# Dividing the attention outputs by their softmax sums after the products instead of before them

## Chip, cores and metric

One core of one Trainium2 chip runs the whole program. The metric is the device time of one execution in microseconds (us). The kernel before took 2548.91 us as the median of three runs (2546.77 to 2551.94).

## What is computed

A decoder trunk of two layers on 1024 positions and 1024 channels, in float32. Each layer projects the normalised input, runs 16 attention heads in three kinds (A: six heads with dilated windows, B: six heads with latent keys and values, C: four differential heads), projects the 1024 channels of all heads with `w_o`, adds the input, and ends with an up and a down projection. The part that matters here:

```python
for layer in range(DEPTH):
    ...
    out_a = mixer_dilated(qa, ka, va, cos64, sin64)
    out_b = mixer_mla(cq, ckv, kr, ...)
    out_c = mixer_diff(qc, kc, vc, ...)
    mixed = jnp.concatenate([out_a, out_b, out_c], axis=-1)
    x = x + mixed @ w_o[layer]
    u = rmsnorm(x, ln2_g[layer]) @ w_up[layer]
    x = x + jnp.square(jax.nn.relu(u)) @ w_down[layer]
```

For a head of kind A or B the output of query i is sum over j of exp(s_ij) v_j, divided by sum over j of exp(s_ij). The kernel computes A's mixture of three windows as one such softmax with a weighted mask.

## The kernel before

**Split products.** Every float32 matrix is split into a high and a low part of TensorE's float32 form (names with `h` and `l`: `mixh`, `mixl`, `ph`, `pl`, `h_wo`, `l_wo`), and a product is three matmuls: high x high, high x low, low x high. The splits keep ScalarE (ACT), GpSimd (POOL) and VectorE (DVE) busy beside TensorE (PE).

**Who sets the order.** The program is first recorded: every operation is noted with its tiles (L179). `order()` (L256) then schedules the noted operations with estimated costs (`cost`, L240); where an operation may run on more than one engine, `WAYS` (L50) lists them (s is ACT, g POOL, v DVE). `replay()` (L409) issues each engine's instructions in that order, so every instruction in the trace has the line L418. On one engine instructions run strictly in the issued order, and the queue of SyncE (SP), which issues all DMAs, is in order too. SBUF is divided into rings of slots per tag (`SLOTS`, L32): a tile takes the next slot of its tag and must wait until the tile that held it has been read. Tags spoken of here are `pp` (5 slots of 128x512), `ms`, `mx` and `oo` (2 slots each) and `pw` (5).

**The heads.** Heads run in the order A0, A1, C0 to C3, A2 to A5, B0 to B5 (`CHUNKS`, `units`), each in four groups of two 128-query blocks. `PLAN` places the other work of the layer beside them. For a query block, `scores` (L804) makes the scores on PE, a masked minimum on DVE (written to `p`, minimum in `w`), the exponential with its sum on ACT, a reciprocal of the sum on DVE (128x1), and the division of the whole row block `p` on POOL:

```python
nc.scalar.activation(p, p, AF.Exp, bias=w[:, z:z + 1], scale=-1.0, accum_out=tot)
if mi == 0:
    if coef is None:
        nc.vector.reciprocal(w[:, 3:4], tot)
        copy("norm", p, p, w[:, 3:4])
```

One group later `values` (L849) turns `p` on PE (`ptp`), splits it into `ph` (ACT) and `pl` (DVE), both in `pp`, and multiplies with the split values into a PSUM bank `o`, whose rows 0 to 63 and 64 to 127 hold two partial sums. `o_sum` (L892) copies both halves with ACT (64x512 each), adds them on POOL and stores the sum to `mix_dram`, twice per head.

While a pair of A heads runs, the keys and queries of the next pair are prepared: POOL multiplies and splits them (`tm_kA`, `tm_qA`), and PE turns them (`pt_kA`).

**The output projection.** Its input rows f = 0 to 7 (128 channels each, a pair of heads; 0 to 2 are A, 3 to 5 are B, 6 and 7 are C) are taken in the groups (6, 0), (7, 1), (2, 3, 4) and (5). `project_load` (L1195) loads the weights and, per f and half z, one 128x512 tile `mixr` from `mix_dram` into `pp`; POOL rounds it to `mixh`, DVE subtracts to `mixl`. The first two groups run beside the B heads. The last two follow the attention: for the first four row tiles t the sums `po_2` of all three f of group (2, 3, 4) are opened in eight PSUM banks, then f = 5 closes them; DVE adds them to `xr`.

```python
raw = tl("pp", [P, 512], f"mixr_{L}_{f}_{z}")
nc.sync.dma_start(raw, mix_dram[L * D + f * P:L * D + (f + 1) * P, cs])
hi_pool(mh[:, cs], raw)
lo_dve(ml[:, cs], raw, mh[:, cs])
```

Of the kernel before, what the change touches and what calls it, by code (L numbers as in the profile page):

```python
# [17 lines left out]
P = 128  # L18
S = 1024
# [27 lines left out]
LAG = 3  # L47
DEEP = 6000.0

WAYS = {'hi': 'g', 'hiact': 's', 'lo': 'vg', 'lop': 'g', 'evac': 'sv', 'norm': 'g', 'osum': 's', 'oadd': 'g', 'lsc': 'gs', 'rope': 'v', 'sq': 's', 'fadd': 'gv', 'fhi': 'sg', 'flo': 'vg', 'fnorm': 'sg', 'fevac': 'sv', 'fsnap': 's', 'fsq': 'sv'}  # L50
SHARED = 0.5

BLOCKS = (0, 4, 8, 12, 15)
# [368 lines left out]
def tile_trunk(  # L422
# [14 lines left out]
    def tl(tag, shape, name, dt=F32):  # L437
        assert 4 * math.prod(shape[1:]) <= SLOTS[tag][0]
        return nc.tile(pool, shape, dt, name, tag, SLOTS[tag][1])
# [25 lines left out]
    def copy(kind, o, i, scale=None):  # L465

        ways = []
        for z in WAYS[kind]:
            if z == "s":
                ways.append(("scalar", "activation", (o, i, AF.Copy), dict(scale=1.0 if scale is None else scale)))  # L470
            elif z == "v":
                ways.append(("vector", "tensor_copy", (o, i), {}) if scale is None else ("vector", "tensor_scalar", (o, i, scale, None, ALU.mult), {}))
            else:
                ways.append(("gpsimd", "tensor_scalar", (o, i, 1.0, 0.0, ALU.mult, ALU.add) if scale is None else (o, i, scale, 1.0, ALU.mult, ALU.mult), {}))
        nc.either(*ways)
# [46 lines left out]
    hl_dram = nc.tile(dram, [DEPTH * NT, P, D], F32, "hl_dram")  # L522
    cq_dram = nc.tile(dram, [DEPTH * S, 512], F32, "cq_dram")
    mix_dram = nc.tile(dram, [DEPTH * D, S], F32, "mix_dram")

    def rstd_of(y, ssq, n, eps, w, nm):

# [45 lines left out]
    for L in range(DEPTH):  # L573
# [153 lines left out]
        def mix_tile(f, g):  # L727
            if (f, g) not in mixf:
                mixf[f, g] = tl("mx", [P, 512], f"mix_{L}_{f}_{g}")
            return mixf[f, g]  # L730

        def mix_out(f, g, src, r0=0, n=P):

            nc.sync.dma_start(mix_dram[L * D + f * P + r0:L * D + f * P + r0 + n, g * 512:(g + 1) * 512], src)
# [69 lines left out]
        def scores(hd, g):  # L804

            maps, scale, nm = hd["maps"], hd["scale"], hd["nm"]
            hd["P"][g] = [None, None]
            cur = {}

            def piece(i, mi, z, c0, m):  # L810
                W = (i + 1) * P
                passes, coef = maps[mi]
                if c0 == 0:
                    cur["w"] = st(f"w_{nm}_{i}_{mi}")
                    cur["p"] = tl("pw", [P, W], f"p_{nm}_{i}_{mi}")
                w, p = cur["w"], cur["p"]
                s = bank("s", f"s_{nm}_{i}_{mi}_{c0}")
                n = max(256, m)
                for pi, (lq, rk) in enumerate(passes):
                    mm(s[:, 0:n], lq[:, i * P:(i + 1) * P], rk[:, c0:c0 + n], pi == 0, pi == len(passes) - 1)  # L820
                nc.vector.tensor_tensor_reduce(out=p[:, c0:c0 + m], in0=s[:, 0:m], in1=hd["mask"](W, c0, m), scale=-scale,
                                               scalar=w[:, 0:1] if z else BIG, op0=ALU.add, op1=ALU.min, accum_out=w[:, z:z + 1])
                if c0 + m < W:
                    return
                tot = hd["tot"][mi][:, i] if "tot" in hd else w[:, 2:3]
                nc.scalar.activation(p, p, AF.Exp, bias=w[:, z:z + 1], scale=-1.0, accum_out=tot)
                if mi == 0:
                    if coef is None:
                        nc.vector.reciprocal(w[:, 3:4], tot)
                        copy("norm", p, p, w[:, 3:4])  # L830
                    hd["P"][g][i % 2] = p
                else:

                    prev = hd["P"][g][i % 2]
                    nc.vector.reciprocal(w[:, 3:4], tot)
                    nc.vector.scalar_tensor_tensor(w[:, 4:5], w[:, 3:4], hd["tot"][0][:, i], coef, ALU.mult, ALU.mult)
                    nc.vector.scalar_tensor_tensor(prev, p, w[:, 4:5], prev, ALU.mult, ALU.add)

            bl = []
            for i in (2 * g, 2 * g + 1):  # L840
                for mi in range(len(maps)):
                    W = (i + 1) * P
                    cuts = [0, W] if W <= 512 else [0, hd.get("cut", 384), W] if W == 640 else [0, 512, W]
                    for z in range(len(cuts) - 1):
                        c0, m = cuts[z], cuts[z + 1] - cuts[z]
                        bl.append((len(maps[mi][0]) * max(256, m) * 0.42, lambda i=i, mi=mi, z=z, c0=c0, m=m: piece(i, mi, z, c0, m)))
            return bl
# [44 lines left out]
        def o_sum(g, o, f, par, nm):  # L892

            tmp = tl("oo", [P, 512], f"ot_{nm}_{g}")
            rows = slice(64 * par, 64 * par + 64)
            dst = tl("oo", [P, 512], f"od_{nm}_{g}")[rows, :] if f < 6 else mix_tile(f, g)[rows, :]
            copy("osum", tmp[rows, :], o[64:128, :])
            copy("osum", dst, o[0:64, :])
            pair("oadd", dst, dst, tmp[rows, :], ALU.add)
            if f < 6:  # L900
                mix_out(f, g, dst, 64 * par, 64)

        def fin_mix(f, par, nm):
            return lambda g, o: o_sum(g, o, f, par, nm)

        def mask_a(W, c0, m):
            return maska[:, S - W + c0:S - W + c0 + m]
# [7 lines left out]
        def prep_a(h):  # L915
            i, par = h // 2, h % 2
            qa, ka, va = heads[f"A{i}"]
            nm = f"A{L}{h}"
            c = slice(64 * par, 64 * par + 64)
            qs = tl("stk", [P, S], f"qs_{nm}", F32R)  # L920
            k1s = tl("stk", [P, S], f"k1s_{nm}", F32R)
            k2s = tl("stk", [P, S], f"k2s_{nm}", F32R)

            def two(src):
                def f(o, ts_):
                    hi_pool(o[:, :, 0:64], src[:, ts_, c])
                    lo_dve(o[:, :, 64:128], src[:, ts_, c], o[:, :, 0:64])
                return f

            def keys(cs, pt):  # L930
                hi_act(k1s[:, cs], pt)
                for z in range(2):
                    nc.sync.dma_start(k2s[64 * z:64 * z + 64, cs].bitcast(F32), k1s[64 - 64 * z:128 - 64 * z, cs].bitcast(F32))

            k = turned(f"k{nm}", two(ka), keys)
            q = turned(f"q{nm}", two(qa), lambda cs, pt: hi_act(qs[:, cs], pt))
            bl = zipped(k[0], k[1], q[0], q[1])
            return bl, dict(maps=[([(qs, k1s), (qs, k2s)], None)], mask=mask_a, scale=SC_A, nm=nm, P={},
                            v=make_v(va[:, :, c], par, nm), fin=fin_mix(i, par, nm))


        bx = {}
# [136 lines left out]
        def prep_b(h):  # L1079
            i, j = h // 2, h % 2  # L1080
            nm = f"B{L}{h}"
            qh, ql = [z[:96] for z in pairs[i][0][j]]
            kh, kl = [Halves(*z) for z in pairs[i][1][j]]
            return [], dict(maps=[([(qh, kh), (qh, kl), (ql, kh)], None)], mask=mask_c, scale=SC_B, nm=nm, P={}, cut=512,
                            v=make_v(bx["V"][:, :, 64 * h:64 * h + 64], j, nm), fin=fin_mix(3 + i, j, nm))

        cst = {}

# [106 lines left out]
        def project_load(gi):  # L1195

            ws, mx = [], []
            if gi == 0:
                for t in range(NT):
                    xs[t] = x_tile(t, f"xr_{L}_{t}")  # L1200
                    src = x[0] if L == 0 else xl_dram
                    nc.sync.dma_start(xs[t], src[t * P:(t + 1) * P, :])
            for f in groups[gi]:
                sc = cst["sg2"] if f >= 6 else None
                ws.append([split(w_o[L, f * P:(f + 1) * P, z * 512:(z + 1) * 512], f"wo_{L}_{f}_{z}", sc) for z in range(2)])
                tag = MIX[f]
                mh = tl(tag, [P, S], f"mixh_{L}_{f}", F32R)
                ml = tl(tag, [P, S], f"mixl_{L}_{f}", F32R)
                for z in range(2):
                    cs = slice(z * 512, (z + 1) * 512)  # L1210
                    raw = tl("pp", [P, 512], f"mixr_{L}_{f}_{z}")
                    nc.sync.dma_start(raw, mix_dram[L * D + f * P:L * D + (f + 1) * P, cs])
                    hi_pool(mh[:, cs], raw)
                    lo_dve(ml[:, cs], raw, mh[:, cs])
                mx.append((mh, ml))
            return ws, mx
# [503 lines left out]
```

## Time and profile before

| what | us |
|---|---|
| median of three runs | 2548.91 |
| the profiled execution | 2549.46 |
| its span in the trace | 2547.70 |
| PE busy | 2473.8 (97% of the span) |
| DVE busy | 2069.9 (81%) |
| ACT busy | 1238.3 (49%) |
| POOL busy | 920.2 (36%) |
| mean granted TensorE clock | 0.991 of full speed |

The span lies 1.76 us under the profiled execution's own time, and that execution 0.55 us over the median. Busy shares are averages over the whole program. A change in one stage is read from that stage's own window: how much of it PE was idle, what ended each idle stretch, and the granted clock there.

### The profile page before, as it was taken

The numbers are of one execution on the slowest core, as the hardware profiler recorded it, in microseconds if no ns is written. First come the engines' busy times: TensorE is split into PE (matmuls) and PEld (weight loads), VectorE is DVE, ScalarE is ACT, GpSimd is POOL, SyncE is SP. The second block draws the span as 40 slices with busy tenths as digits, with TensorE's granted clock in tenths as the row PEclk, the third lists the DMA queues.
The fourth block names the chain that finished last, engine by engine and source line by source line (L and its number), as shares of the span: only waits on it lengthen the run. The fifth ranks groups of instructions, "written<-read, shape, count | busy, mean of one in ns | idle before, by whom it ended". The sixth has DMA issues, their size and how long they took to land. (4 is left out here: it accounts for less than half of the span.)

```text
span 2547.7 us, 39227 instructions
## 1 busy us (share of the span) xinstructions
PE 2473.8 (97%) x12808; PEld 2077.0 (82%) x12808; DVE 2069.9 (81%) x4326; ACT 1238.3 (49%) x2548; POOL 920.2 (36%) x1078
## 2 busy tenths in 40 slices
PE   8999999999999999999999999999999999999996
PEld 7878889988788887888888778898887888788885
DVE  4679998887877777989856799988778777789989
ACT  3566667743544444323235666677345444333332
POOL 2344355653200114455323343556330001144543
PEclk9999999999999999999999999999999999999998
DMA  8354433433354457544453554344243444765332
GB/s 255 96 142 135 112 94 94 135 93 130 116 172 164 153 197 262 156 145 120 137 164 97 133 137 122 81 110 142 78 142 129 163 159 146 268 210 157 112 120 79
DMA packets 292636, 360.58 MB, mean 142 GB/s; under 512 B 48848, under 2 KB 172112, under 8 KB 292432
## 3 DMA queue, kind: packets, MB, share of 16 engines
q1 hardware_dynamic: 292432, 358.08, 45.6%
q8 instruction: 102, 1.67, 0.3%
q14 instruction: 102, 0.84, 0.1%
HBM read 231.63 MB, written 94.90 MB: 128 GB/s over the span
## 5 line engine op out<-in xcount | busy, mean ns | idle before, releaser
L418 PE MATMUL pd<-hb,ha 128*128 128x512 f32 x2520 | 577.2, 390 | 5.4 <-DVE hb L418 3.5
L418 PE MATMUL pu<-xc,uh 128*128 128x512 f32 x1792 | 552.7, 393 | 13.4 <-ACT ua L418 8.2
L418 PEld LDWEIGHTS pd<-hb,ha 128*128 128x128 f32 x2520 | 471.4, 188 | 109.6 <-DVE hb L418 8.3
L418 PEld LDWEIGHTS pu<-xc,uh 128*128 128x128 f32 x1792 | 336.9, 189 | 90.0 <-ACT ua L418 10.0
L418 PE MATMUL pu<-xc,ul 128*128 128x512 f32 x896 | 346.7, 393 | 0.0
L418 PEld LDWEIGHTS pu<-xc,ul 128*128 128x128 f32 x896 | 169.6, 189 | 36.8 <-DVE ul L418 0.8
L418 DVE TENSOR_TENSOR ha<-hr,ha 128x512 fp32r<-128x512 f32 x151 | 145.6, 967 | 24.8 <-POOL ha L418 23.0
L418 POOL TENSOR_SCALAR ha<-hr 128x512 fp32r<-128x512 f32 x90 | 74.1, 824 | 245.1 <-DVE xd L418 94.8
L418 ACT ACTIVATE hb<-wt 128x512 fp32r<-128x512 f32 x98 | 60.4, 627 | 184.4 <-PE pd L418 157.3
L418 ACT ACTIVATE uh<-su 128x512 fp32r<-128x512 f32 x124 | 77.5, 631 | 138.4 <-PE pu L418 121.6
L418 ACT ACTIVATE hb<-wd 128x512 fp32r<-128x512 f32 x82 | 50.4, 627 | 158.8 <-PE pd L418 157.3
L418 ACT ACTIVATE p_C<-p_C,w_C 128x256 f32<-128x256 f32 (+7 forms) x128 | 98.9, 773 | 55.3 <-DVE w_C L418 54.7
L418 POOL TENSOR_SCALAR p_A<-p_A,w_A 128x128 f32<-128x128 f32 (+3 forms) x96 | 77.2, 806 | 116.5 <-DVE w_A L418 83.6
L418 POOL TENSOR_SCALAR uh<-wu 128x512 fp32r<-128x512 f32 x16 | 13.3, 832 | 280.1 <-PE pu L418 168.5
L418 DVE TENSOR_TENSOR hb<-wt,hb 128x512 fp32r<-128x512 f32 x105 | 109.7, 1061 | 0.7 <-ACT hb L418 0.5
L418 DVE TENSOR_TENSOR xd<-pd,xd 128x512 f32<-128x512 f32 x128 | 86.8, 682 | 26.6 <-PE pd L418 26.5
L418 PE MATMUL pf_C<-wh_C,hh 128*128 128x512 f32 x256 | 104.7, 413 | 1.7 <-POOL wh_C L418 0.9
L418 PE MATMUL pf_C<-wl_C,hh 128*128 128x512 f32 x256 | 104.4, 408 | 0.4 <-DVE wl_C L418 0.3
L418 PE MATMUL po<-h_wo,mixh 128*128 128x512 f32 x256 | 103.3, 403 | 1.0 <-POOL h_wo L418 1.0
L418 POOL TENSOR_SCALAR p_B<-p_B,w_B 128x384 f32<-128x384 f32 (+4 forms) x96 | 74.4, 780 | 79.8 <-DVE w_B L418 62.3
L418 PE MATMUL pf_A<-wh_A,hh 128*128 128x512 f32 (+1 forms) x256 | 100.0, 395 | 3.0 <-DVE w_C L418 2.1
L418 PE MATMUL pf_C<-wh_C,hs_C 128*128 128x512 f32 x256 | 101.8, 401 | 0.7 <-DMA hs_C<-hl_dram 0.7
(343 smaller groups left out, 6775.8 us busy)
## 6 DMA issues: line engine op xcount, KB each, us to landing
hr<-hc_dram SPq DMA_DIRECT2D x210, 256.0 KB, 2.8
wu<-in_w_up_dram SPq DMA_DIRECT2D x148, 256.0 KB, 3.0
hc_dram<-hc SPq DMA_DIRECT2D x120, 256.0 KB, 2.3
wd<-in_w_down_dram SPq DMA_DIRECT2D x120, 256.0 KB, 3.7
hs_C<-hl_dram SPq DMA_DIRECT2D x32, 512.0 KB, 3.5
hs_A<-hl_dram SPq DMA_DIRECT2D x32, 512.0 KB, 3.5
hc_dram<-ua SPq DMA_DIRECT2D x60, 256.0 KB, 2.3
hl_dram<-hl SPq DMA_DIRECT2D x16, 512.0 KB, 5.6
```

The source lines that it names most:

```text
L418: getattr(getattr(self.nc, eng), method)(*[real(v) for v in args], **{k: real(v) for k, v in kw.items()})
```

## The change

The division by the softmax sum leaves the attention of heads A and B. `scores` only collects the sums of a head in one tile `sums` (128x8); after the head's last block one reciprocal (128x8) is taken and stored to a new DRAM tensor `rs_dram`, transposed, so that a row of it holds a head's 1024 reciprocals. `fin_mix` copies both halves of `o` with one ACT instruction (128x512) and stores each half to its own place in `half_dram`; the addition on POOL is gone. `project_load` now loads, for f < 6, both halves (`mixr` into tag `ms`, `mixo` into tag `mx`) and the reciprocals, broadcast over 64 partitions each by two DMAs (`mixs`, tag `pp`); one addition and one multiplication (128x512, on DVE or POOL) make what `mixr` held before. For f = 6 and 7 only the tag of `mixr` changes.

```diff
-... 'norm': 'g', ...
+... 'onorm': 'vg', ...
...
-                tot = hd["tot"][mi][:, i] if "tot" in hd else w[:, 2:3]
+                tot = hd["tot"][mi][i] if coef is None else hd["tot"][mi][:, i]
                 nc.scalar.activation(p, p, AF.Exp, bias=w[:, z:z + 1], scale=-1.0, accum_out=tot)
                 if mi == 0:
-                    if coef is None:
-                        nc.vector.reciprocal(w[:, 3:4], tot)
-                        copy("norm", p, p, w[:, 3:4])
                     hd["P"][g][i % 2] = p
+                    if coef is None and i == NT - 1:
+                        r = one([P, NT], "rsum")
+                        nc.vector.reciprocal(r, hd["sums"])
+                        nc.sync.dma_start(rs_dram[hd["row"]].rearrange("(t p) -> p t", p=P), r)
...
-            return lambda g, o: o_sum(g, o, f, par, nm)
+            def fin(g, o):
+                tmp = tl("oo", [P, 512], f"ot_{nm}_{g}")
+                copy("osum", tmp, o)
+                for z in range(2):
+                    r = (L * 6 + f) * P + 64 * par
+                    nc.sync.dma_start(half_dram[z, r:r + 64, g * 512:(g + 1) * 512], tmp[64 * z:64 * z + 64, :])
+            return fin
...
-                    raw = tl("pp", [P, 512], f"mixr_{L}_{f}_{z}")
-                    nc.sync.dma_start(raw, mix_dram[L * D + f * P:L * D + (f + 1) * P, cs])
+                    raw = tl("ms", [P, 512], f"mixr_{L}_{f}_{z}")
+                    if f < 6:
+                        r = slice((L * 6 + f) * P, (L * 6 + f + 1) * P)
+                        nc.sync.dma_start(raw, half_dram[0, r, cs])
+                        other, rs = tl("mx", [P, 512], f"mixo_{L}_{f}_{z}"), tl("pp", [P, 512], f"mixs_{L}_{f}_{z}")
+                        nc.sync.dma_start(other, half_dram[1, r, cs])
+                        for j in range(2):
+                            src = rs_dram[(L * 6 + f) * 2 + j:(L * 6 + f) * 2 + j + 1, cs]
+                            nc.sync.dma_start(rs[64 * j:64 * j + 64, :], src.broadcast_to([64, 512]))
+                        pair("onorm", raw, raw, other, ALU.add)
+                        pair("onorm", raw, raw, rs, ALU.mult)
+                    else:
+                        nc.sync.dma_start(raw, mix_dram[L * D + f * P:L * D + (f + 1) * P, cs])
```

With other operations the scheduler issues other orders. Three places show it. The names end in layer-local indices and a serial number, which differs between the two kernels.

POOL beside head A4 of layer 0, while the next pair's keys are prepared (`p_A_4`, `p_A_5` are row blocks of scores, `od_A` the sum of an output's halves). Before:

```order
L418 TENSOR_SCALAR p_A_4_0_4539<-p_A_4_0_4539,w_A_4_0_4540 128x640
L418 TENSOR_SCALAR wqrh_4618<-wqrr_1_4261,gq 128x192
L418 TENSOR_SCALAR tm_kA_1_4652<-qkv_A_3653 128x4x64
L418 TENSOR_SCALAR tm_qA_0_4661<-qkv_A_3653 128x4x64
L418 TENSOR_TENSOR od_A_0_4650<-od_A_0_4650,ot_A_0_4638 64x512
L418 TENSOR_TENSOR tm_kA_1_4652<-qkv_A_3653,tm_kA_1_4652 128x4x64
L418 TENSOR_TENSOR tm_qA_0_4661<-qkv_A_3653,tm_qA_0_4661 128x4x64
L418 TENSOR_SCALAR p_A_5_0_4640<-p_A_5_0_4640,w_A_5_0_4641 128x768
```

The same place now:

```order
L418 TENSOR_SCALAR cc_7_4536<-cc_7_4536,rl 128x384
L418 TENSOR_SCALAR tm_kA_1_4579<-qkv_A_3623 128x4x64
L418 TENSOR_SCALAR tm_qA_0_4586<-qkv_A_3623 128x4x64
L418 TENSOR_TENSOR tm_kA_1_4579<-qkv_A_3623,tm_kA_1_4579 128x4x64
L418 TENSOR_TENSOR tm_qA_0_4586<-qkv_A_3623,tm_qA_0_4586 128x4x64
```

The four instructions of the key and query preparation stand next to each other; the two divisions and the addition between them are gone.

PE at the first sums of the last two projection groups, layer 0. Before:

```order
L418 MATMUL po_2_0_0_7785<-h_wo_2_0_7493,mixh_2_7750 128x512
L418 MATMUL po_2_0_0_7785<-l_wo_2_0_7528,mixh_2_7750 128x512
L418 MATMUL po_2_0_0_7785<-h_wo_2_0_7493,mixl_2_7756 128x512
L418 MATMUL po_2_0_0_7785<-h_wo_3_0_7589,mixh_3_7774 128x512
L418 MATMUL po_2_0_0_7785<-l_wo_3_0_7606,mixh_3_7774 128x512
```

Now:

```order
L418 MATMUL po_2_0_0_7635<-h_wo_2_0_7331,mixh_2_7600 128x512
L418 MATMUL po_2_0_0_7635<-l_wo_2_0_7342,mixh_2_7600 128x512
...
L418 MATMUL po_2_0_0_7635<-h_wo_3_0_7436,mixh_3_7690 128x512
...
L418 MATMUL po_2_0_0_7635<-h_wo_4_0_7610,mixh_4_7749 128x512
...
L418 MATMUL po_2_0_0_7635<-h_wo_5_0_7699,mixh_5_7790 128x512
```

Before, f = 3 follows after three matmuls of f = 2 and the banks are filled nearly one after the other. Now all 24 matmuls of f = 2 for the eight banks come first, then 24 of f = 3, 24 of f = 4 and 24 of f = 5: the first row of each f here stands 24 instructions behind that of the f before it.

SP's queue at the end of layer 0's attention. Before:

```order
L418 DMA mixr_2_0_7723<-mix_dram 128x512
L418 DMA mixr_2_1_7725<-mix_dram 128x512
L418 DMA mixr_3_0_7728<-mix_dram 128x512
L418 DMA mixr_3_1_7737<-mix_dram 128x512
L418 DMA mixr_4_0_7744<-mix_dram 128x512
L418 DMA mix_dram<-od_B_1_7747 64x512
```

Now:

```order
L418 DMA half_dram<-ot_B_1_7586 64x512 x2
L418 DMA mixs_3_1_7592<-rs_dram 64x512
L418 DMA mixs_4_0_7614<-rs_dram 64x512 x2
L418 DMA mixs_4_1_7625<-rs_dram 64x512 x2
L418 DMA mixr_3_0_7633<-half_dram 128x512
L418 DMA mixs_5_0_7639<-rs_dram 64x512 x2
L418 DMA wu_0_1_0_7648<-in_w_up_dram 128x4x128
L418 DMA mixr_3_1_7658<-half_dram 128x512
```

Before, five loads of `mixr` stand in the queue ahead of the last output's store (tag `pp` has five slots). Now `mixr` of f = 3 comes after that store and after the broadcasts of f = 4, since tag `ms` has two slots and both hold f = 2 until its low parts have been taken.

## Rows read from the trace of the kernel before

**Rows 1.** The page's part 1: busy time and share of the span.
```profile
PE 2473.8 (97%) x12808; PEld 2077.0 (82%) x12808; DVE 2069.9 (81%) x4326; ACT 1238.3 (49%) x2548; POOL 920.2 (36%) x1078
```

**Rows 2.** Stages: PE, PEld, DVE, ACT, POOL busy us (instructions), TensorE clock, DMA.
```profile
300.00:395.00 95.00, 89.16 (x589) 81.40 (x588) 87.39 (x276) 62.61 (x138) 52.45 (x73) 0.96 0.34 94
...
395.00:590.00 195.00, 193.86 (x1328) 173.64 (x1328) 157.82 (x417) 124.13 (x266) 103.28 (x126) 1.00 0.40 113
...
1555.00:1650.00 95.00, 89.79 (x590) 80.45 (x589) 87.87 (x276) 63.69 (x138) 52.94 (x74) 0.98 0.36 98
```

**Rows 3.** Waits of PE, 355 to 395 us: us in total, times, longest.
```profile
PE pt_kA L418 <- POOL tm_kA L418: 1.8, 1, 1.8
...
PE s_A L418 <- DVE w_A L418: 1.4, 1, 1.4
```

**Rows 4.** Waits of PE, whole span.
```profile
PE pt_kA L418 <- POOL tm_kA L418: 5.7, 3, 2.2
...
PE ptp_A L418 <- POOL p_A L418: 1.5, 3, 0.8
```

**Rows 5.** Timeline of POOL in layer 0, head A4: start, us, instruction, idle before.
```profile
369.85 1.23 POOL L418 TENSOR_SCALAR p_A<-p_A,w_A 128x640 f32<-128x640 f32 x1
...
373.54 1.27 POOL L418 TENSOR_TENSOR od_A<-od_A,ot_A 64x512 f32<-64x512 f32 x1 [1.32 <-issue]
...
374.88 0.73 POOL L418 TENSOR_TENSOR tm_kA<-qkv_A,tm_kA 128x256 fp32r<-128x256 f32 x1
```

**Rows 6.** Timeline of PE at its longest wait for tm_kA.
```profile
69.91 1.12 PE L418 MATMUL pt_kA<-ident,tm_kA 128*128 128x128 f32 x4 [2.18 <-POOL tm_kA L418]
```

**Rows 7.** Windows as in rows 2: 10 us of either layer.
```profile
375.00:385.00 10.00, 8.57 (x45) 7.72 (x46) 9.80 (x23) 4.96 (x11) 7.54 (x11) 0.66 0.34 70
...
1630.00:1640.00 10.00, 7.82 (x43) 5.97 (x41) 9.39 (x20) 5.74 (x12) 8.08 (x12) 0.83 0.35 75
```

**Rows 8.** Groups by line and shape: count, busy us, mean ns, idle before.
```profile
L418 DVE RECIPROCAL w_A<-w_A 128x1 f32<-128x1 f32 x96 | 14.8, 155 | 15.3 <-ACT p_A L418 14.8
...
L418 POOL TENSOR_TENSOR od_A<-od_A,ot_A 64x512 f32<-64x512 f32 x24 | 31.5, 1311 | 15.4 <-ACT od_A L418 7.6 <-issue 5.1 <-PE ptp_B L418 1.3
...
L418 DVE TENSOR_TENSOR xr<-po,xr 128x512 f32<-128x512 f32 x96 | 65.1, 685 | 38.4 <-PE po L418 38.0
...
L418 DVE TENSOR_TENSOR mixl<-mixr,mixh 128x512 fp32r<-128x512 f32 x32 | 27.8, 902 | 0.0
```

**Rows 9.** The page's part 5: the division of heads A on POOL, shapes together.
```profile
L418 POOL TENSOR_SCALAR p_A<-p_A,w_A 128x128 f32<-128x128 f32 (+3 forms) x96 | 77.2, 806 | 116.5 <-DVE w_A L418 83.6
```

**Rows 10.** Windows as in rows 2: a stretch of nothing but 512-column products.
```profile
750.00:800.00 50.00, 50.00 (x222) 41.07 (x221) 37.56 (x59) 24.34 (x42) 0.62 (x1) 1.00 0.51 171
```

**Rows 11.** Tile mixr: count, duration ns min/median/max; DMA landing.
```profile
L418 POOL TENSOR_SCALAR mixh<-mixr x32: 611/822/1093, 522.8 to 1853.5; 128x512 fp32r<-128x512 f32 x32
...
L418 DVE TENSOR_TENSOR mixl<-mixr,mixh x32: 676/994/1100, 523.9 to 1855.0; 128x512 fp32r<-128x512 f32 x32
...
DMA to landing us min/median/max: 2.5/3.4/4.4
```

**Rows 12.** Timeline of PE at the end of layer 0's attention.
```profile
583.71 0.28 PE L418 MATMUL o_B<-pl_B,vhl_B 128*128 128x256 f32 x1
...
590.85 0.39 PE L418 MATMUL po<-h_wo,mixh 128*128 128x512 f32 x1
...
596.35 0.50 PE L418 MATMUL po<-h_wo,mixh 128*128 128x512 f32 x1 [0.58 <-POOL h_wo L418]
```

**Rows 13.** Timeline of ACT in the same place.
```profile
577.74 0.19 ACT L418 ACTIVATION_READ_ACCUMULATOR p_B<-p_B,w_B 128x1 f32 x1
...
586.46 0.59 ACT L418 ACTIVATE ot_B<-o_B 64x512 f32<-64x512 f32 x1 [1.38 <-PE o_B L418]
```

**Rows 14.** DMA issues: count, KB each, median us to landing.
```profile
mix_dram<-od_A SPq DMA_DIRECT2D x24, 128.0 KB, 2.2
...
g<-in_ln_g_dram SPq DMA_DIRECT2D x4, 4.0 KB, 4.1
```

More of the change, by code (lines that the diff above doesn't have):

```diff
@@ L48 @@
 DEEP = 6000.0
-WAYS = {'hi': 'g', 'hiact': 's', 'lo': 'vg', 'lop': 'g', 'evac': 'sv', 'norm': 'g', 'osum': 's', 'oadd': 'g', 'lsc': 'gs', 'rope': 'v', 'sq': 's', 'fadd': 'gv', 'fhi': 'sg', 'flo': 'vg', 'fnorm': 'sg', 'fevac': 'sv', 'fsnap': 's', 'fsq': 'sv'}
+WAYS = {'hi': 'g', 'hiact': 's', 'lo': 'vg', 'lop': 'g', 'evac': 'sv', 'onorm': 'vg', 'osum': 's', 'oadd': 'g', 'lsc': 'gs', 'rope': 'v', 'sq': 's', 'fadd': 'gv', 'fhi': 'sg', 'flo': 'vg', 'fnorm': 'sg', 'fevac': 'sv', 'fsnap': 's', 'fsq': 'sv'}
 SHARED = 0.5
@@ L524, in tile_trunk @@
     mix_dram = nc.tile(dram, [DEPTH * D, S], F32, "mix_dram")
+    half_dram = nc.tile(dram, [2, DEPTH * 6 * P, S], F32, "half_dram")
+    rs_dram = nc.tile(dram, [DEPTH * 12, S], F32, "rs_dram")
     def rstd_of(y, ssq, n, eps, w, nm):
@@ L895, in o_sum @@
             rows = slice(64 * par, 64 * par + 64)
-            dst = tl("oo", [P, 512], f"od_{nm}_{g}")[rows, :] if f < 6 else mix_tile(f, g)[rows, :]
+            dst = mix_tile(f, g)[rows, :]
             copy("osum", tmp[rows, :], o[64:128, :])
@@ L899, in o_sum, with summed @@
             pair("oadd", dst, dst, tmp[rows, :], ALU.add)
-            if f < 6:
-                mix_out(f, g, dst, 64 * par, 64)
         def fin_mix(f, par, nm):
-            return lambda g, o: o_sum(g, o, f, par, nm)
+            def fin(g, o):
[5 more added lines that the diff above has]
+            return fin
+        def summed(h, f):
+            t = one([P, NT], "sums")
+            return dict(sums=t, tot=[[t[:, i:i + 1] for i in range(NT)]], row=(L * 6 + f) * 2 + h % 2)
         def mask_a(W, c0, m):
@@ L938, in prep_a @@
             return bl, dict(maps=[([(qs, k1s), (qs, k2s)], None)], mask=mask_a, scale=SC_A, nm=nm, P={},
-                            v=make_v(va[:, :, c], par, nm), fin=fin_mix(i, par, nm))
+                            v=make_v(va[:, :, c], par, nm), fin=fin_mix(i, par, nm), **summed(h, i))
         bx = {}
@@ L1084, in prep_b @@
             return [], dict(maps=[([(qh, kh), (qh, kl), (ql, kh)], None)], mask=mask_c, scale=SC_B, nm=nm, P={}, cut=512,
-                            v=make_v(bx["V"][:, :, 64 * h:64 * h + 64], j, nm), fin=fin_mix(3 + i, j, nm))
+                            v=make_v(bx["V"][:, :, 64 * h:64 * h + 64], j, nm), fin=fin_mix(3 + i, j, nm), **summed(h, 3 + i))
         cst = {}
```

## The prediction, made before the changed kernel ran

> **What bounds the kernel now.** I read the page's busy shares first, then windows over the stages, then PE's waits in the stages where PE is not full, then the timelines at those places. PE is busy for 97% of the span, DVE for 81%, POOL for 36% [rows 1]: the change takes work from POOL, DVE and ACT, none of which bounds the whole. So it can pay only where PE waits for one of them. The windows say where the edited code runs and PE has room: heads A2 to A5 of either layer, 300 to 395 us and 1555 to 1650 us, with PE busy for 89.16 and 89.79 of 95 us. In layer 0's B heads PE is busy for 193.86 of 195 us [rows 2], so there is almost nothing to win, and anything added there must stay off PE's path.
>
> In layer 0's A stretch PE waits 1.8 us once for `tm_kA` from POOL and 1.4 us once for `w_A`, the row minimum, from DVE [rows 3]; over the whole span it waits 5.7 us in three times for `tm_kA` and 1.5 us in three times for the divided `p_A`, both from POOL [rows 4]. The POOL timeline shows how the edited instructions come into this: at head A4 a division (1.23 us from 369.85) and the addition of an output's halves (1.27 us from 373.54, after 1.32 us idle) run ahead of the second half of `tm_kA` at 374.88 [rows 5], all in one in-order queue. Just behind, from 375 to 385 us, the granted clock is 0.66; in layer 1 it is 0.83 from 1630 to 1640 us, both with PE less than nine tenths busy [rows 7]. Of the two levels of 1.2 and 2.4 GHz a part of these stretches ran at the lower.
>
> **Part one: what is taken away.** The divisions of heads A fill 77.2 us of POOL (96 of 806 ns) [rows 9] and the additions of A's outputs 31.5 us (24 of 1311 ns); heads B have about as much. DVE loses 192 reciprocals of 155 ns [rows 8], and ACT gets 48 copies of 128x512 for 96 of 64x512. Off PE's path all of that is worth nothing: PE's own work hides it. On the path I count:
>
> - Layer 0, A heads: the 1.8 us wait for `tm_kA` goes, since nothing stands ahead of it on POOL any more. Of the 1.4 us wait for DVE two reciprocals (0.3 us) go; the row minima stay. The low clock costs 10 x (1 - 0.66) = 3.4 us; I give back two thirds (2.3), because DVE's wait, which stays, can bring it about too. Sum 4.4.
> - Layer 1: of the 5.7 us for `tm_kA`, 1.8 is layer 0's, and 2.2 falls at 69.9 us [rows 6], in the preparation of the first A heads, ahead of any division; 1.7 is left and goes. Clock 10 x (1 - 0.83) = 1.7, two thirds 1.1. Sum 2.8.
> - The waits for `p_A` itself: 1.5 in all.
> - B heads: PE is idle for 195 - 193.86 = 1.1 us a layer; I take half, so 1.1 for both.
>
> Together 9.8 us. The least is 3.5 us (the waits for `tm_kA`, 1.8 + 1.7, go and something late takes all the rest), the most about 18 us: all of the 5.8 and 5.2 us that PE is idle in the two windows, the two clock losses in full (3.4 and 1.7), and 1.1 twice.
>
> **Part two: what is added in the attention.** 24 reciprocals of 128x8 on DVE, in place of 192, save. Each of the 48 output copies has the columns of one of the two that it replaces. SP issues 144 DMAs more; its queue is only late where a load waits for a slot, which is part three. The stores of halves are 128 KB like those of today, which land in 2.2 us [rows 14], and nobody needs them soon, except the last. The loads, additions and multiplications of f = 0 and 1 run beside the B heads, 16 DVE instructions for both layers, under the DVE instructions that go. I cost these edits at nothing; their cover is a PE that is full in the B heads and whose work of `project` is there as filler.
>
> **Part three: what is added at the end of the attention.** Here a two-slot ring takes the place of a five-slot one. Before, four to five loads of `mixr` are under way before the attention ends, and PE starts `po_2` at 590.85 and waits 0.58 us once, at 596.35 [rows 12]. Now f = 3 can be loaded only when f = 2's tiles are consumed, f = 4 after f = 3, f = 5 after f = 4. One turn of this ring: the load of `mixr` lands in 3.4 us, POOL's `mixh` takes 822 ns [rows 11], DVE's `mixl` 902 ns [rows 8]. An addition or multiplication of 128x512 float32 from SBUF on DVE does not occur in the trace. The nearest rows are `mixl` (two SBUF inputs, 902 ns) and `xr` (one input from PSUM, 685 ns) [rows 8]; I take `mixl`'s, which has the same operands. So one turn is 3.4 + 0.9 + 0.9 + 0.8 + 0.9 = 7.0 us (rounded up from 6.9). PE needs for the 24 matmuls of an f, at 50 us / 222 = 0.225 us each [rows 10], 5.4 us. Each of f = 3, 4 and 5 then makes PE wait about 1.6 us.
>
> The first turn, worked out in time: the last product of the attention's second-last step ends at 583.71 + 0.28 = 584.0 [rows 12], which frees the `pp` slots for f = 2's reciprocals. Two issues of about 0.45 us and 2.2 us to land (as a 128 KB transfer [rows 14], the nearest row) make 587.1. Two multiplications, two `xr` additions that stand between them in DVE's order, `mixh` and a `mixl` bring 591.2; `mixr` of f = 3 lands 3.4 later, at 594.6; after the rest of DVE's queue there, addition, multiplication and `mixh` give 597.9. PE began `po_2` at 590.85 and is through f = 2 at 590.85 + 5.4 = 596.25: a wait of 1.65. With 1.6 twice more and today's 0.6 taken off, 4.25 us a layer, 8.5 in all.
>
> Its bounds: with the shortest durations (landing 2.5, `xr`'s 0.68 twice, `mixh` 0.61, `mixl` 0.68) a turn is 5.15 us, PE waits for nothing, and today's 0.6 us a layer goes too: -1.2. With the longest (4.4, 1.10 three times, 1.09) it is 8.8 us, three waits of 3.4 less 0.6 are 9.6 a layer: +19.2.
>
> `mixl`'s own spread, 676 to 1100 ns for one shape [rows 11], is what decides between those ends for the DVE part. The Trainium skill (SBUF — State Buffer, on the port pair that DVE and GpSimd share) says that a DVE instruction with two SBUF inputs and a GpSimd instruction that reads SBUF exclude each other for their whole length. By that rule the additions and multiplications would be as short as the shortest rows wherever POOL is idle, and with POOL's work gone the sum would be nearer its lower end. No row here shows one of them alone.
>
> **Sum.** 8.5 - 9.8 = -1.3 us on the profiled execution's 2549.46, so 2548.2; the median of the runs is 0.55 lower, so 2547.6. A measurement of this kernel can tell about 0.2%, 5.1 us, from no change: by the sum, the two parts nearly cancel.
>
> **Rivals.**
>
> - *The ring keeps up.* A turn at or under 5.4 us leaves PE no wait at the end; then -9.8 - 1.2 and the 0.55 give 2537.9. For it: shortest durations, and PE at the transition may run slower than 0.225 us a matmul (0.39 and 0.50 us are single rows there [rows 12]). Against: the median landing alone is 3.4 us, and four instructions stand behind it. A faster outcome also comes from a middling turn with a gain near its upper end. Chance 0.33.
> - *The ring decides, and it is slower.* DVE also adds the closed banks to `xr` and splits weights there, and SP stands in order behind stores that wait for ACT: the last output's copy starts at 586.46 [rows 13]. With a turn of 8.0 us three waits of 2.6 less 0.6 make 7.2 a layer, 14.4; if of the gain only half comes (4.9, because DVE's minima remain the last releaser in the A heads), 2549.46 + 14.4 - 4.9 - 0.55 = 2558.4. It is slower by more than 0.2% from a turn of 7.3 us with half the gain, or 8.1 us with all of it. Chance 0.20.
> - *The sums arrive late.* `rs_dram` gets 1024 single numbers by one store. The last exponential of B5 is read out at 577.74 [rows 13], and the broadcast that needs it, for f = 5, stands in SP's queue behind `mixr` of f = 3, issued at about 591: a cover of 13 us. The nearest row, the load of as many single numbers for `g`, lands in 4.1 us [rows 14]. Only a store of over 13 us delays anything: at 18 us it is 5 us a layer, 10 on top of the sum, 2557.6. Chance 0.05. The Trainium skill (DMA: Bandwidth & Descriptors, Specifications) puts the least transfer at full rate at 512 bytes and says that below it the engine reads, modifies and writes, which speaks against such a store. No row here shows a store of single numbers.
>
> That the change doesn't do what it says can be left out: the order shows the divisions and additions gone from POOL.
>
> **How the numbers follow.** The forecast, both parts near their middle, has 0.42. The range reaches from 2536, a little under the ring that keeps up, to 2559, the ring that decides; outside lie the gain's upper end without a wait and the longest turns. Its own part of the range, with turns of 6.2 to 7.6 us, is 2543 to 2552. Faster by over 0.2% takes the first rival: 0.33. Slower takes the second and third: 0.25. Within: 0.42.
>
> **What would show it.** Right: PE's waits for `tm_kA` and `p_A` on POOL are down to the one at 69.9 us, and the clock from 375 to 385 us is above 0.85. Right: PE waits about 1.6 us at the first matmul of f = 3, 4 and 5 in each layer, and `mixr` lands in some 3.4 us, with 0.9 us for addition and multiplication. Wrong: no such waits (first rival), or longer ones, with DVE or the load in the chain behind them (second); an `rs_dram` store that lands after more than 13 us (third); or waits for `w_A` on DVE that have grown by what POOL's have lost, and a clock that still falls there, which would halve the gain.

## The result and the profile after

The changed kernel takes 2644.22 us (median of four runs, 2641.91 to 2653.52) against 2547.84 us: a ratio of 1.0381, 95% interval 1.0364 to 1.0398. It is 96 us slower where 2547.6 was forecast. The profiled execution has a span of 2651.3 us; it is the slowest of the four, some 9 us above their median, so the spans of the two traces differ by more than the medians do.

The page's busy time by engine, to be read beside [rows 1]:

```profile
PE 2502.8 (94%) x12808; PEld 2103.1 (79%) x12808; DVE 2057.3 (78%) x4204; ACT 1206.1 (45%) x2500; POOL 699.4 (26%) x840
```

DVE, ACT and POOL have less work than before, POOL by 221 us, as the change meant. PE has the same 12808 matmuls and a smaller share of a longer span. So no engine has become the bound: something makes PE wait. Windows over the stages, with the columns of [rows 2] and, for the two long ones, the same bounds as there:

```profile
300.00:395.00 95.00, 88.45 (x572) 80.09 (x571) 82.99 (x262) 59.02 (x126) 36.36 (x51) 0.98 0.41 109
395.00:590.00 195.00, 168.07 (x1159) 154.39 (x1158) 127.19 (x327) 107.06 (x240) 30.45 (x47) 0.91 0.51 112
1555.00:1650.00 95.00, 91.46 (x552) 78.59 (x551) 87.60 (x276) 63.67 (x154) 28.80 (x37) 1.00 0.42 119
```

In layer 0's A heads, where a gain was expected, PE is as busy as before (88.45 and 89.16 of 95 us); in layer 1 the work has shifted by then, and the window doesn't hold the same work. In layer 0's B heads PE had been idle for 1.1 us of 195 [rows 2]; now it is idle for 26.9, and the clock is 0.91 instead of 1.00. PE's waits, whole span (us in total, times, longest), show no common culprit by name:

```profile
PE po L418 <- POOL mixh L418: 15.9, 6, 5.5
PE pkn_B L418 <- DVE ql_B L418: 15.8, 2, 9.7
PE pf_C L418 <- POOL wh_C L418: 14.3, 2, 7.5
PE ptp_B L418 <- DVE pl_B L418: 13.1, 2, 6.8
PE s_B L418 <- issue: 6.8, 2, 3.9
...
PE pt_kA L418 <- POOL tm_kA L418: 2.2, 1, 2.2
```

`ql_B`, `wh_C` and `pl_B` are not touched by the change, and each is waited for just twice. What the forecast counted as gain is there: of the waits for `tm_kA` [rows 4] only the one at 69.9 us is left, and `p_A` on POOL is gone. What the new waits have in common is found one view further. SP's timeline (start, us, issue) around one store of a head's reciprocals, and PE, PEld, DVE, ACT, POOL, clock, share of the DMA engines and GB/s in windows of 2 us behind it:

```profile
454.27 0.54 SPq L418 DMA_DIRECT2D rs_dram<-rsum  x1
454.91 0.95 SPq L418 DMA_DIRECT2D kh_B<-kh_B  x1
...
457.87 0.53 SPq L418 DMA_DIRECT2D mixr<-mix_dram  x1
465.72 0.53 SPq L418 DMA_DIRECT2D kh_B<-kr  x1
```

```profile
458.00:460.00 2.00, 2.00 (x20) 2.00 (x19) 1.12 (x2) 1.24 (x3) 0.00 (x0) 1.00 1.08 64
460.00:462.00 2.00, 2.00 (x13) 1.50 (x11) 1.30 (x3) 0.81 (x2) 0.00 (x0) 1.00 0.41 15
462.00:464.00 2.00, 0.06 (x1) 0.00 (x0) 0.69 (x1) 0.82 (x3) 0.00 (x0) 1.00 0.40 19
464.00:466.00 2.00, 1.03 (x7) 0.98 (x8) 0.49 (x1) 0.00 (x0) 0.00 (x0) 1.00 0.39 27
466.00:468.00 2.00, 2.00 (x19) 2.00 (x18) 1.08 (x5) 1.15 (x2) 0.00 (x0) 1.00 0.59 152
```

The store is issued at 454.27; the transfers behind it are issued at a half to one microsecond each up to 457.87. Then little moves: 64, 15, 19 and 27 GB/s from 458 to 466 us, and 152 after it. SP issues no more until 465.72, and from 462 to 464 us PE is busy for 0.06 us of 2, DVE and ACT for 0.69 and 0.82, POOL not at all: their inputs had not come. The engine names in the list of waits are merely those that stood last in such a gap. There are 12 of these stores in a layer.

How much of the 103.6 us between the two profiled spans lies where, I read from PE's timeline by four marks in each layer: its first matmul into `pj` (input projection), its last into `s_A` (end of the scores of A and C), its last into `o_B`, its last into `po`, and the first `pj` of the next layer or the last matmul of the program's `pdl`. The table, in us, also has the experiments below:

| kernel | A, C 0 | B 0 | po 0 | rest 0 | A, C 1 | B 1 | po 1 | rest 1 |
|---|---|---|---|---|---|---|---|---|
| before | 423.9 | 154.3 | 55.1 | 638.6 | 408.6 | 153.9 | 55.0 | 630.5 |
| after | 432.9 | 188.4 | 59.1 | 637.3 | 428.9 | 184.9 | 61.5 | 629.8 |
| e2 stores alone | 442.6 | 180.5 | 59.1 | 639.5 | 425.6 | 182.9 | 60.0 | 628.7 |
| e8 spread | 423.1 | 154.2 | 55.0 | 637.4 | 408.8 | 154.6 | 55.0 | 631.0 |
| e13 spread, 64 bytes | 425.4 | 154.0 | 55.5 | 639.0 | 411.0 | 154.0 | 55.1 | 630.8 |
| e9 loads instead | 421.5 | 154.6 | 55.1 | 636.8 | 407.8 | 154.0 | 55.2 | 631.8 |
| e1 runs of 32 bytes | 422.1 | 154.2 | 60.7 | 637.6 | 409.1 | 151.0 | 62.6 | 630.0 |
| e4 turned | 423.6 | 154.4 | 61.0 | 636.9 | 409.4 | 153.7 | 59.9 | 629.1 |
| e5 halves alone | 423.7 | 154.6 | 53.8 | 640.0 | 409.2 | 154.1 | 53.8 | 630.2 |
| e10 mixs in tmp | 422.7 | 158.0 | 54.2 | 639.5 | 411.1 | 157.6 | 54.2 | 631.3 |
| e11 and on POOL | 421.5 | 155.2 | 54.2 | 639.8 | 411.8 | 154.5 | 54.2 | 628.9 |
| e6 division alone | 421.1 | 155.8 | 54.2 | 641.0 | 406.7 | 156.1 | 54.2 | 630.9 |
| e12 and on POOL | 422.1 | 154.4 | 54.2 | 638.8 | 409.2 | 154.3 | 54.2 | 631.1 |
| e14 heads A alone | 423.0 | 159.5 | 54.2 | 639.3 | 406.0 | 160.8 | 54.2 | 629.5 |

Each row is one profiled execution. e8, e13 and e9 issue the same instructions in the same order on every engine (e9 has a load where the others have a store), and the division is untouched in them. Still they lie up to 3.9 us apart in the columns A, C, up to 2.2 in rest, and up to 0.6 in B and po: so much is chance. From before to after the attention takes it nearly all: 9.0 + 34.1 in layer 0, 20.3 + 31.0 in layer 1. The end of the attention, which the forecast was about, adds 4.0 and 6.5.

### The profile page after: what moved, and what is told of

Its sections match the earlier page's. It is cut to its first block, busy times and chain, and to the rows that moved or that the text cites. A ratio compares the mean times of both kernels' runs of the same rounds, so it can differ in the third digit from the quotient of the medians.

```text
span 2651.3 us, 38756 instructions
## 1 busy us (share of the span) xinstructions
PE 2502.8 (94%) x12808; PEld 2103.1 (79%) x12808; DVE 2057.3 (78%) x4204; ACT 1206.1 (45%) x2500; POOL 699.4 (26%) x840
## 5 line engine op out<-in xcount | busy, mean ns | idle before, releaser
L418 ACT ACTIVATE hb<-wt 128x512 fp32r<-128x512 f32 x98 | 60.3, 627 | 181.0 <-PE pd L418 154.5
L418 ACT ACTIVATE p_B<-p_B,w_B 128x128 f32<-128x128 f32 (+3 forms) x96 | 74.2, 773 | 112.2 <-DVE w_B L418 110.7
L418 PE MATMUL po<-h_wo,mixl 128*128 128x512 f32 x256 | 103.6, 413 | 2.8 <-DVE mixl L418 2.8
L418 DVE TENSOR_TENSOR pl_A<-ptp_A,ph_A 128x512 fp32r<-128x512 f32 (+1 forms) x120 | 74.7, 632 | 40.1 <-ACT ph_A L418 37.1
L418 PE MATMUL po<-l_wo,mixh 128*128 128x512 f32 x256 | 105.4, 412 | 0.0
```

The costliest lines, as they stand in the source:

```text
L418: getattr(getattr(self.nc, eng), method)(*[real(v) for v in args], **{k: real(v) for k, v in kw.items()})
```

## The experiments

Two theories stood against each other. S: the stores of single numbers keep the other transfers away. R: the ring, the halves and the many DMAs in one queue cost it.

**e1: the same change, the store in runs of 32 bytes.** The program is the changed one, instruction for instruction.

```diff
-nc.sync.dma_start(rs_dram[hd["row"]].rearrange("(t p) -> p t", p=P), r)
+nc.sync.dma_start(rs_dram[hd["row"]].rearrange("(p t) -> p t", p=P), r)
```

> The changed kernel with one edit: each reciprocal store writes 128 runs of 32 bytes instead of 1024 single numbers, in the same 4 KB row of DRAM; the order of instructions is the same on every engine, so outputs are divided by the reciprocals of other positions. Theory S (a store of single numbers keeps the other transfers away for several us, 24 times): the time falls by 85 to 105 us, to 2538 to 2560, and PE's waits in heads A and B of both layers fall to those of the kernel before. Rival R (the two-slot ring, the halves and 144 more DMAs in one in-order queue cost it): the time stays above 2620. In between, 2560 to 2620: both take part.

Measured: 2556.99 us, ratio to before 1.0033 (1.0022 to 1.0045). One line takes back 87 of the 96 us, inside S's band, and by the table the attention is back at the values of before (layer 1's B heads 2.9 us below). S holds, R falls as the main cause; what is left, 7.6 us, comes from the columns po, +5.6 and +7.6, less what the others lose.

**e2: the kernel before, plus the stores alone.**

```diff
+                    if coef is None and i == NT - 1:
+                        nc.sync.dma_start(rs_dram[hd["row"]].rearrange("(t p) -> p t", p=P), hd["sums"])
```

> The kernel before, with its division in place, plus 24 stores of the sums of a head as 1024 single numbers each, which nobody reads. Theory S: slower by 60 to 110 us (2.5 to 4.5 us a store), with stretches of some 8 us behind each store in which hardly any bytes move. Rival R: within 10 us of the kernel before.

Measured: 2642.32 us, ratio 1.0365 (1.0335 to 1.0394). With nothing else of the change nearly the whole slowdown is there, in both of its two executions: 93 us, a mean of 3.9 us a store. Theory R is not needed for it.

**e4: the change, complete, with the reciprocals turned on PE.**

```diff
-nc.sync.dma_start(rs_dram[hd["row"]].rearrange("(t p) -> p t", p=P), r)
+pt = bank("pt", f"rst_{nm}")
+nc.tensor.transpose(pt[0:NT, 0:P], r, ident)
+q = one([P, 2, P], "cqs")[0:NT, 0]
+copy("evac", q, pt[0:NT, 0:P])
+nc.sync.dma_start(rs_dram[hd["row"]].rearrange("(t p) -> t p", p=P), q)
```

> The changed kernel, complete, but the reciprocals of a head (128x8) are turned by one transposition on PE to 8x128, copied to SBUF and stored as 8 runs of 512 bytes; 24 transpositions and 24 copies more. Theory S: 2538 to 2560, as with runs of 32 bytes, and if the forecast of the rest holds, 2543 to 2552. Rival R: above 2620.

Measured: 2557.34 us, ratio 1.0030 (1.0018 to 1.0042). The result stays that of the whole computation, so the slowdown was not needed for what the change does; but it is still 8 us above before, above the 2552 that the forecast of the rest allowed.

**e8 and e13: the stores alone, each number 512 or 64 bytes from the next.** The instructions and their order are those of e2 on every engine, and so are order and number of transfers.

```diff
-rs_dram[hd["row"]].rearrange("(t p) -> p t", p=P)
+rs_dram[hd["row"]].rearrange("(t p s) -> p t s", p=P, s=128)[:, :, 0]
```

(in e13 s=16, with `rs_dram` larger accordingly).

> The kernel before plus the same 24 unread stores of 1024 single numbers, each number now 512 bytes from the next in DRAM; the order of instructions is that of the run with the stores alone. If it is writing single numbers next to each other that holds the transfers up (writes into one piece of memory wait for one another): within 25 us of the kernel before. If each single number costs, wherever it goes: 2625 to 2660 as with the stores alone.

> The kernel before plus the 24 unread stores of 1024 single numbers, each 64 bytes from the next (they were 4 and 512 bytes apart in the two runs before; same order of instructions). If only writes into the same 64 bytes wait for one another: 2545 to 2556, as at 512 bytes. If pieces of up to 512 bytes matter: in between, 2560 to 2640.

Measured: 2550.42 us, ratio 1.0009 (0.9999 to 1.0019) at 512 bytes; 2551.32 us, 1.0007 (0.9996 to 1.0018) at 64. The packets of e2 and e8 are the same to the last one, and so is their count under 512 bytes:

```profile
DMA packets 317596, 360.68 MB, mean 136 GB/s; under 512 B 73808, under 2 KB 197072, under 8 KB 317392
...
rs_dram<-sums SPq DMA_DIRECT2D x24, 4.0 KB
```

```profile
DMA packets 317596, 360.68 MB, mean 142 GB/s; under 512 B 73808, under 2 KB 197072, under 8 KB 317392
...
rs_dram<-sums SPq DMA_DIRECT2D x24, 4.0 KB, 2.9
```

24,960 small packets more than before cost nothing that could be measured when no two of the numbers go into the same 64 bytes; packed together, 16 to 64 bytes, they cost 93 us. (The last figure of a row is the median from issue to landing, 2.9 us in e8; in e2 the profile gives no landing for any transfer.) The traces show the same. From 2 to 10 us behind the issue of the same store, e2 (first row) and e8 run the same number of instructions on every engine, and DMA moves 23 and 82 GB/s:

```profile
1418.60:1426.60 8.00, 8.00 (x54) 7.12 (x53) 5.20 (x14) 5.19 (x14) 0.86 (x2) 1.00 0.13 23
1366.30:1374.30 8.00, 8.00 (x54) 7.11 (x53) 5.20 (x14) 5.18 (x14) 0.86 (x2) 1.00 0.24 82
```

Over all 24 stores, from 3 to 10 us behind the issue, the median rate is 20 GB/s in e2, 88 in e8 and 86 in e13. Behind this one store PE loses nothing; a store costs time where something waits for a transfer. So it isn't the number of packets, nor their size alone: it is single writes close to each other. At which distance between 4 and 64 bytes the cost begins no run shows, nor whether e1's runs of 32 bytes, two into each 64, cost nothing that could be measured because they are longer or because they are fewer.

**e9: loads of single numbers instead of the stores.**

```diff
-nc.sync.dma_start(rs_dram[hd["row"]].rearrange("(t p) -> p t", p=P), hd["sums"])
+nc.sync.dma_start(hd["sums"], x[0, hd["row"]].rearrange("(t p) -> p t", p=P))
```

> The kernel before plus 24 loads of 1024 single numbers in place of the stores, in the same layout and at the same places (into the tile of the sums once it has been read). If transfers of single numbers as such hold up the others: 2600 to 2660. If only writes do: within 20 us of the kernel before.

Measured: 2549.95 us, ratio 1.0009 (0.9997 to 1.0021), landing in 2.3 us. Reading 1024 adjacent numbers one by one cost nothing that could be measured; writing them did. The row that the forecast used for a bound, a load [rows 14], said nothing on a store.

**e5 and e6: one part of the change each.** e5 has the halves without the division; e6 the turned division without the halves, `mixr` in `ms` and `mx`, `mixs` in `tmp`.

```diff
+                    if coef is None:
+                        nc.vector.reciprocal(w[:, 3:4], tot)
+                        copy("norm", p, p, w[:, 3:4])
...
-                        pair("onorm", raw, raw, rs, ALU.mult)
```

is e5 against the changed kernel, in part (the stores and loads of the reciprocals go too), and e6 against e4, in part:

```diff
-            copy("osum", tmp, o)
...
+            copy("osum", tmp[rows, :], o[64:128, :])
+            copy("osum", dst, o[0:64, :])
+            pair("oadd", dst, dst, tmp[rows, :], ALU.add)
+            mix_out(f, g, dst, 64 * par, 64)
...
-                        pair("onorm", raw, raw, other, ALU.add)
```

> One part of the change alone: both halves of an output are stored and added where the projection loads them, through the two-slot rings; the division stays on POOL in the attention, and there are no reciprocal stores or loads. Theory S: 2540 to 2562 (ring costs of 0 to 19 us, little gain). Rival R: 2600 or more, since the ring, the halves and most of the added DMAs are in it.

> The other part of the change alone: the division by the sums at the projection, with turned reciprocals, but an output's halves added on POOL in the attention as before and stored once; mixr in ms and mx (one per half), mixs in tmp. If the gain in the A heads comes from the divisions that leave POOL: 2536 to 2546, and PE no longer waits for p_A or tm_kA on POOL except the one at 69.9 us. If the additions and the stores' order carry it: 2546 to 2554.

Measured: e5 2549.27 us, ratio 0.9997 (0.9986 to 1.0009); e6 2548.70 us, 0.9998 (0.9986 to 1.0009). Neither part changes the time by anything that could be measured. e6 lies in the band that gave the gain to the additions, but e5, which has them, gains nothing either. In e6 the A and C heads are 2.8 and 1.9 us shorter, which chance can also do, and the B heads 1.5 and 2.2 us longer, which is more than chance in that column. In e5 the division is still on POOL, PE waits longer for `p_A` than before (9.0 us in 6 times against 1.5 in 3 [rows 4]), and still the A and C heads take what they took before: a wait that goes is not yet time that is won.

**e10: mixs in the ring tmp.** Against e4 only the tag of `mixs` changes.

```diff
-rs = tl("pp", [P, 512], f"mixs_{L}_{f}_{z}")
+rs = tl("tmp", [P, 512], f"mixs_{L}_{f}_{z}")
```

> The kernel with turned reciprocals (8 runs of 512 bytes), complete, with one tag changed: the broadcast reciprocals mixs lie in the ring tmp (3 slots) instead of pp (5 slots), which the attention's ph and pl use to its end; the rings of mixr and mixo keep two slots. Theory T (mixs in pp makes every load of f = 2 to 5 wait for the attention's last products): the loads of f = 2 to 4 land during the B heads, PE is full from 590 to 625 us as with halves alone, and the time is 2535 to 2545. Rival U (one turn of the two-slot rings is longer than PE's work on one f, as the prediction had it): the waits before f = 3, 4 and 5 stay and the time is 2552 to 2560.

Measured: 2555.29 us, ratio 1.0032 (1.0020 to 1.0044). Both theories were half right. Windows of the end of layer 0's attention in the kernel before, in e4 and in e10 (columns of [rows 2]):

```profile
590.00:625.00 35.00, 34.15 (x158) 27.82 (x156) 26.01 (x60) 10.41 (x20) 12.88 (x18) 1.00 0.39 133
```

```profile
590.00:625.00 35.00, 29.79 (x115) 22.89 (x115) 24.13 (x45) 4.61 (x8) 6.48 (x10) 0.90 0.73 228
```

```profile
590.00:625.00 35.00, 35.00 (x164) 29.16 (x163) 21.86 (x54) 9.23 (x18) 6.76 (x11) 1.00 0.45 151
```

PE is idle for 5.2 of 35 us, with the clock at 0.90, where `mixs` shares `pp` with `ph` and `pl`, and never where it lies in `tmp`: with the same two slots for `mixr` there are no waits at the end, so they were due to that tag, as T said. (e5, with the two-slot rings and no `mixs`, has the same: 53.8 us in the columns po.) But the time stays. Against e4 the columns po lose 6.8 and 5.7 us, the B heads take 3.6 and 3.9 more, and the columns A, C and rest together 5.6 more, which chance can do.

**e11 and e12: the added work at the projection on POOL alone**, from e10 and e6.

```diff
-'onorm': 'vg'
+'onorm': 'g'
```

> The complete kernel with turned reciprocals and mixs in tmp, with one more edit: the additions and multiplications at the projection run on POOL alone, not on DVE or POOL. With mixs in tmp the end of the attention was mended but the B heads had grown by 3.7 us a layer. If DVE's added instructions among the B heads are that cost: 2542 to 2550, and last o_B some 3 us earlier in each layer. If DVE is not the cause: 2552 to 2558.

> The division alone at the projection (halves added in the attention as before), with its multiplications on POOL alone. B heads had grown by 1.5 and 2.1 us in the two layers with them on DVE or POOL. If DVE is the cause: 2541 to 2547. If not: 2547 to 2551.

Measured: e11 2551.61 us, ratio 1.0016 (1.0007 to 1.0025); e12 2547.29 us, 0.9994 (0.9985 to 1.0003). In both, the B heads are back within 0.9 us of before. In e10 PE waits 4.9 us in two times for `w_B` on DVE; in the kernel before it waits 0.6 us for it, and in e11 not at all. That fits DVE's share of the added work as the cost, but with another engine the scheduler also issues another order, and no run tells the two apart. e12, at 2547.29, stands 0.29 us beyond the band for DVE as the cause, and e11 misses its own by 2 us. e12 is the fastest version of the division at the projection, and not to be told from the kernel before.

**e14: the division at the projection for heads A alone.** Against e6, in part; heads B have the division of before, and the multiplication at the projection is left for f < 3.

```diff
-                            ..., fin=fin_mix(3 + i, j, nm), **summed(h, 3 + i))
+                            ..., fin=fin_mix(3 + i, j, nm))
```

> The division at the projection for heads A alone (f = 0 to 2, turned reciprocals, halves added in the attention as before); heads B divide in the attention as in the kernel before. It should keep the 3.2 and 1.8 us that the A heads gained and the 1 us at the end of the attention, and lose the cost in the B heads: 2541 to 2546. If the A heads' gain does not last to the end of the layer: 2547 to 2551.

Measured: 2558.23 us, ratio 1.0044 (1.0030 to 1.0057). A miss: the A and C heads of layer 1 are 2.6 us shorter, but the B heads, which should run as before, take 5.2 and 6.9 us more. This speaks against the number of added DVE instructions as the whole cost: beside layer 0's B heads there are 5, against 7 in e6. The order in which the scheduler puts the work beside them is another one. PE waits there for `ph_B` on ACT (3.2 us in two times) and `p_B` on POOL (2.5 in three); which instruction costs it stays open.

## Why the prediction was wrong

**The step that failed: the stores of the reciprocals were costed at nothing.** Part two of the prediction counted them among SP's 144 DMAs that are "only late where a load waits for a slot". The third rival named the right instruction and priced it wrongly: it asked when the store itself lands, gave it 13 us of cover and a chance of 0.05. No trace gives the landing of such a store, but the cover was there: in layer 0 the broadcasts for f = 5 are issued 16.7 us behind the store (638.69 and 622.03). What the runs showed in its place is that the store holds up the other transfers behind it, at 454.27 us for some 8 us, so that its own lateness is beside the point: 24 stores at a mean of 3.9 us make 93 us (e2), and with the stores in runs of 32 bytes the same program takes 2556.99 instead of 2644.22 (e1). The range was too narrow because this price had no bound from any row: the nearest, a load of single numbers, was taken for one.

**The Trainium skill (DMA: Bandwidth & Descriptors, Specifications)** says that a transfer below 512 bytes makes the DMA engine read, modify and write. It was cited beside the rival as speaking against the store. The page gives no price for it. The runs agree that such a store can be ruinous, but show that the size of a transfer alone doesn't tell: the same 24,576 writes of 4 bytes cost nothing that can be told when they lie 64 bytes apart (e13, 1.0007), and 93 us when they are adjacent (e2).

**The gain: 9.8 us forecast, about 4 measured or less, and in the A heads none of it clear of chance.** In e1, which has the order of the changed kernel and not its stores of single numbers, A, C and B together are 1.9 us shorter in layer 0 and 2.4 in layer 1; in e4 0.2 shorter and 0.6 longer. The waits named in it did go, and the low clock with them, but PE's idle time did not:

```profile
375.00:385.00 10.00, 8.27 (x67) 7.37 (x66) 8.47 (x24) 6.88 (x16) 4.51 (x8) 1.00 0.46 97
1630.00:1640.00 10.00, 7.14 (x48) 5.13 (x47) 10.00 (x23) 7.25 (x15) 7.40 (x12) 1.00 0.41 105
```

Against [rows 7] the granted clock is 1.00 in both, and PE is busy for 8.27 and 7.14 us of 10, no more than before. Over the long windows of [rows 2] it idles 5.5 and 5.7 us of 95 in e1, and 5.8 and 5.2 before. DVE is busy for 10.00 us of 10 in the second; before it had been 9.80 and 9.39 [rows 7], which the forecast quoted for the clock alone. PE's waits in e1 from 355 to 395 us:

```profile
PE pt_qA L418 <- DVE w_A L418: 1.3, 1, 1.3
...
PE s_A L418 <- DVE w_A L418: 0.4, 1, 0.4
```

The second rival had this as its condition ("DVE's minima remain the last releaser in the A heads"). By these rows DVE is late there once POOL no longer is. Which wait ended last there was read; what is late next was not worked out.

**The end of the attention: 8.5 us forecast, 13.2 in e1 (5.6 + 7.6) and 10.8 in e4.** Here the mechanism was right and the size too small. In layer 0 PE waits at the first matmul of f = 3 and of f = 4, 5.15 us together; 4.85 had been worked out for three waits, so that the sums agree is partly luck (in layer 1 the waits are 2.14, 1.20 and 4.46 us):

```profile
596.91 0.50 PE L418 MATMUL po<-h_wo,mixh 128*128 128x512 f32 x1 [2.73 <-POOL mixh L418]
...
606.69 0.50 PE L418 MATMUL po<-h_wo,mixh 128*128 128x512 f32 x1 [2.42 <-POOL mixh L418]
```

What was not counted is the clock, 0.90 in e1 too over the 35 us from 590 to 625, after 1.00 before. Two terms of the turn were off, in opposite ways. SP's issues and DVE's additions in e1 show the loads of `mixr` for f = 3 and f = 4 there:

```profile
590.43 0.53 SPq L418 DMA_DIRECT2D mixr<-half_dram  x1
594.74 0.69 DVE L418 TENSOR_TENSOR mixr<-mixr,mixo 128x512 f32<-128x512 f32 x1 [3.19 <-DMA mixr<-half_dram]
599.50 0.33 SPq L418 DMA_DIRECT2D mixr<-half_dram  x1
604.52 0.69 DVE L418 TENSOR_TENSOR mixr<-mixr,mixo 128x512 f32<-128x512 f32 x1 [0.95 <-DMA mixr<-half_dram]
```

The first load of f = 3 is there at 594.7, as forecast (594.6). But these loads take 4.3 and 5.0 us, not 3.4. The instructions are shorter than the forecast's 0.9, as the tile's rows in e1 show (duration ns min/median/max):

```profile
L418 POOL TENSOR_SCALAR mixh<-mixr x32: 609/618/1022, 463.3 to 1876.8; 128x512 fp32r<-128x512 f32 x32
L418 DVE TENSOR_TENSOR mixl<-mixr,mixh x32: 675/685/1081, 464.1 to 1877.8; 128x512 fp32r<-128x512 f32 x32
...
L418 DVE TENSOR_TENSOR mixr<-mixr,mixs x24: 677/692/1098, 518.9 to 1876.0; 128x512 f32<-128x512 f32 x24
L418 DVE TENSOR_TENSOR mixr<-mixr,mixo x20: 682/691/1120, 494.4 to 1872.5; 128x512 f32<-128x512 f32 x20
...
DMA to landing us min/median/max: 2.5/2.9/6.1
```

By the medians a turn would be 2.9 + 0.69 + 0.69 + 0.62 + 0.69 = 5.6 us, hardly over PE's 5.4; with the load of 5.0 us it is 7.7 or more. The additions and multiplications take 0.69 us, like the shortest `mixl` [rows 11], not 0.90; `mixl`'s median fell from 994 to 685 ns with POOL's work gone. **The Trainium skill (SBUF — State Buffer, on the port pair that DVE and GpSimd share)** says that a DVE instruction with two SBUF inputs and a GpSimd instruction that reads SBUF exclude each other, and the trace agrees with it: in the kernel before, each of the 18 `mixl` of over 900 ns has a POOL instruction running beside it, and the 7 with none take 676 to 685. That the turns fall behind the attention at all comes from `mixs` waiting for `pp`, as the forecast's first turn had it; that the same two slots cost nothing with another tag (e10) it did not see.

**B heads: no cost forecast, and a gain of 0.55 us a layer.** With the stores out of the way they do not get longer (e1: -0.1 and -2.9; e4: +0.1 and -0.2), but only as long as the loads came late: once they come early (e6, e10), the B heads take 1.5 to 3.7 us a layer more, and 0.1 to 0.9 once the added instructions run on POOL (e12, e11).

## What to carry to other kernels

A transposing store that writes a row of DRAM number by number can hold up nearly all DMA traffic of a core for microseconds; the store's own landing time says nothing of that. Turn the tile first and store rows, or at least store short runs (32 bytes were enough in e1): that alone was worth 87 us. Where a price has no row of its own kind (a store bounded by a load), the range has to say so; and before a wait is counted as a gain, look at what the other engines are doing at that moment: one that is busy for 10.00 of 10 us may be late next.

## What the runs showed of the hardware that was not expected

- Why adjacent single writes hold up the transfers no run shows; only the spacing was tried, and with it the stretch of DRAM they cover grew. 1024 writes of 4 bytes into adjacent places: transfers at 15 to 64 GB/s for the 8 us from 458 to 466, a mean of 3.9 us of the program's time each. The same writes 64 or 512 bytes apart: ratios of 1.0007 and 1.0009, with intervals that hold 1. 128 writes of 32 bytes into the same 4 KB: no such stall in e1. 1024 reads of 4 bytes: 2.3 us to landing and no effect that could be measured.
- A window's DMA share can be high while little moves: in the 2 us from 458 us it is 1.08 of the engines at 64 GB/s, which I take to be transfers that are held up and count as busy; in e2's row it is 0.13 at 23 GB/s. The GB/s show the stall, the share need not.
